# Another table of queue orders for a two-layer diffusion backbone on one core

## The chip, the core and the metric

The kernel runs on one NeuronCore of one Trainium2 chip. A core has five engines that run side by side, each through its own list of instructions in order: TensorE (PE, matrix multiplication, with weight loads shown as PEld), VectorE (DVE), ScalarE (ACT), GpSimd (POOL) and SyncE (SP, which here only issues DMA transfers). They wait for each other by semaphores. The metric is device microseconds of the program on that core; lower is better. The kernel before took 1788.57 us (median of three runs, 1785.81 to 1789.31).

## The reference

Two layers over 512 latent tokens and 256 context tokens, 1024 features, all in float32:

```python
# layer 0: neighbourhood attention (8 heads) beside spatial gating, one output projection
q, k, v, u, g = jnp.split(h_lat @ w_in, splits, axis=-1)
a_lat = neighbourhood_attention(heads(q), heads(k), heads(v), heads(kc), heads(vc), rpb)
s_lat = spatial_gating(jax.nn.gelu(u), jax.nn.gelu(g), w_s, b_s)
y_lat = jnp.concatenate([a_lat, s_lat], axis=-1) @ w_out
# layer 1: two-way retention with 8 heads; its state starts from the context
y_lat = retention_output(outs_lat[0] + outs_lat[1], g, gn_g, w_out)
# after each: a gated MLP with a convolution over three tokens
a = dwconv3(h @ w_in, conv_w, conv_b)
gate, up = jnp.split(a, 2, axis=-1)
return (jax.nn.silu(gate) * up) @ w_out
```

Every part is normalised before and after, and shifted, scaled and gated by `silu(c) @ ada_w + ada_b` (called ada below).

## The kernel before

Each float32 operand of a large product is split into a high and a low part that TensorE reads in one pass; a product is then three matmuls (high by high, high by low, low by high, lines 216, 217 and 218 in the helper `mm3`, line 215 where a single helper line issues all), which add into one tile of PSUM. ScalarE writes the high part (line 171) and VectorE the low part (line 172).

The stages follow each other: the start (ada of the first norm, tiles `ad`, lines 266 to 289; transposes of the input, tile `ht`, line 1831; the projection `ug`), spatial gating, attention, output projection, the first MLP, retention, the second MLP. Matmuls of a stage have one width: 512 columns for `ug`, `wf` and `wr`, 256 for `px`, `rn` and the scores, 384 for the first MLP.

Four small kinds of PE instruction differ from these:

- In attention, `weigh` (lines 1144 to 1151) multiplies the transposed weights by the values in plain float32, into a PSUM tile `o` of which one half of the matmuls writes partitions 0 to 63 (lines 1144, 1146, 1148, 1149 and so on as `lo`) and the other half partitions 64 to 127 (`up`): ten instructions a head. Each is recorded as two passes.
- For the context tokens the same function issues four such matmuls a head into `oc` (line 1167), two into each half.
- The first ada products (`ad`, line 266) are in plain float32 too, 32 instructions with two passes each.
- Rows of ada results are turned into columns by transposes with two or four rows (`at` in line 370, `adt` in line 276): 64 instructions.

All other transposes have 128 rows.

The order in which an engine issues is not the order of the Python code. After everything is built, `queue` (line 1849) takes each engine's list, decodes a table `ORDER` for it, and chains the instructions in the order of the table:

```python
for e in LANES:                      # PE, DVE, Activation, Pool, SP
    lane, at, last = lanes[getattr(mybir.EngineType, e)], -1, None
    for _ in lane:
        ...                          # one number z of the table
        at += 1 + (z // 2 if z % 2 == 0 else -(z + 1) // 2)
        if last is not None:
            self.tc.add_manual_dep(lane[at], last.name, sync, reason="queue")
        last = lane[at]
```

A number of 0 means "the next one of the program's own order"; others jump forward or back. The table holds 10,880 places for PE, 2,299 for DVE, 1,746 for ACT, 458 for POOL and 400 for SP. Tiles have their addresses before the table is read, and what waits for what follows from the data and the addresses.

Of the kernel before, what the change touches and what calls it, by code (L numbers as in the profile page):

```python
# [2045 lines left out]
```

## Time and profile before

| | |
|---|---|
| time, median of three runs | 1788.57 us (1785.81, 1788.57, 1789.31) |
| profiled execution, first to last instruction | 1784.0 us (4.6 us under the median; its time as the runs count it is not listed) |
| PE busy | 1748.3 us |
| DVE, ACT, POOL busy | 1388.2, 1017.5, 340.1 us |
| DMA, mean | 142 GB/s |

Times in the profile count from the first instruction. A row of the list in order of time gives the start, the time of one or several merged instructions, the engine, the line, the tile written and the tiles read, the shape (rows by columns of the weights, then what is written) and the count. Matmuls are pipelined, so the time that one takes from the engine is read from the start of one to the start of the next and not from its own duration.

### The profile page before, as it was taken

To read this page: it belongs to the slowest core of one execution; us is meant where nothing else is said; L and a number is where in the kernel's file an instruction comes from. 1 tells how busy PE (TensorE), PEld (TensorE's weight loads), DVE (VectorE), ACT (ScalarE), POOL (GpSimd) and SP (SyncE) were. 2 spreads that over 40 slices of the span, in tenths; PEclk is the share of its full clock that TensorE was granted. 3 is DMA by queue.
4 is the path that set the end of the run, shared out by engine and by line. 5 is a ranking of instruction groups with operands and counts; after the bars stand their busy time and mean duration, and the time that the engine had idled before them with its cause. 6 is when DMAs were issued, how large, how long until landed. Compare 5 with 4: busy or idle time off the path is not lost.

```text
span 1784.0 us, 28774 instructions
## 1 busy us (share of the span) xinstructions
PE 1748.3 (98%) x11024; PEld 1578.7 (88%) x11024; DVE 1388.2 (78%) x2363; ACT 1017.5 (57%) x1882; POOL 340.1 (19%) x462
## 2 busy tenths in 40 slices
PE   7999999999999999999999999999999999999997
PEld 4898888799998999999899998998999789999996
DVE  3887886898887787889867666666655799998887
ACT  6633567776555555655665434433444577766773
POOL 1101322230132322222221001101001200222221
PEclk9999999999999999999999999999999999999999
DMA  8345331364687877886734332332322235887764
GB/s 304 116 133 165 99 110 45 106 180 118 171 174 174 173 174 155 164 178 161 257 126 125 118 113 71 119 95 81 97 71 60 107 122 147 214 216 185 180 145 130
DMA packets 84398, 253.44 MB, mean 142 GB/s; under 512 B 11026, under 2 KB 11538, under 8 KB 84260
## 3 DMA queue, kind: packets, MB, share of 16 engines
q1 hardware_dynamic: 55044, 191.27, 33.7%
q0 software_dynamic: 26912, 51.95, 17.1%
q10 hardware_dynamic: 2304, 8.39, 1.2%
q8 instruction: 86, 1.41, 0.3%
q14 instruction: 52, 0.43, 0.1%
HBM read 191.80 MB, written 39.85 MB: 130 GB/s over the span
## 4 chain that ended last, share of the span: by engine, by line
PE 89%; DVE 5%; ACT 3%; DMA 1%; issue 1%; POOL 1%; SPq 0%; DVEq 0%; POOLq 0%; ACTq 0%
PE px L215 11%; PE wf L216 4%; PE wf L217 4%; PE wf L218 4%; PE rn L217 4%; PE rn L216 4%; PE rn L218 4%; PE py L215 4%; PE px L216 2%; PE px L217 2%; PE px L218 2%; PE py L218 1%; PE py L217 1%; PE py L216 1%; PE ug L216 1%; PE ug L217 1%
## 5 line engine op out<-in xcount | busy, mean ns | idle before, releaser
L326 DVE SCALAR_TENSOR_TENSOR acc<-ar,cs,acc 128x512 f32<-128x512 f32 x256 | 190.5, 758 | 11.1 <-DMA ar<-in_adaw 4.3
L216 PE MATMUL rn<-rwv,h0c 128*128 128x256 f32 x384 | 107.8, 281 | 0.0
L217 PE MATMUL rn<-rwv,h0c 128*128 128x256 f32 x384 | 107.5, 281 | 0.0
L218 PE MATMUL rn<-rwv,h1c 128*128 128x256 f32 x384 | 107.2, 280 | 0.0
L1734 POOL DMA_DIRECT2D yf<-yp x64 | 56.0, 963 | 265.1 <-ACT yp L1730 237.7
L1574 ACT ACTIVATE pre<-px 128x256 f32<-128x256 f32 (+2 forms) x160 | 56.0, 369 | 78.0 <-PE px L215 55.9
L1587 DVE SCALAR_TENSOR_TENSOR cv<-pre,cw,cv 128x769 f32<-128x769 f32 (+1 forms) x88 | 77.3, 882 | 27.5 <-ACT cv L1586 26.9
L1586 ACT ACTIVATE cv<-pre,cw 128x770 f32<-128x770 f32 (+1 forms) x88 | 80.9, 925 | 21.5 <-DVE g L172 11.4
L1730 ACT COPY yp<-wf 128x512 f32<-128x512 f32 x118 | 68.4, 584 | 41.8 <-PE wf L218 34.2
L215 PE MATMUL px<-blk,wb 128*128 128x384 f32 (+1 forms) x480 | 79.2, 309 | 1.1 <-ACT pre L1574 1.1
L215 PE MATMUL px<-hs,wc 128*128 128x384 f32 (+1 forms) x480 | 78.9, 309 | 1.0 <-ACT pre L1574 0.8
L1590 DVE SCALAR_TENSOR_TENSOR cv<-pre,cw,cv 128x769 f32<-128x769 f32 (+1 forms) x88 | 76.8, 881 | 0.9
L215 PEld LDWEIGHTS px<-hs,wc 128*128 128x128 f32 x480 | 73.5, 188 | 4.1 <-ACT pre L1574 1.6
L215 PEld LDWEIGHTS px<-blk,wb 128*128 128x128 f32 x480 | 72.8, 188 | 3.8 <-ACT pre L1574 1.6
L171 ACT ACTIVATE wc<-q 128x512 fp32r<-128x512 f32 x80 | 49.8, 629 | 44.1 <-PE py L215 20.7
L216 PEld LDWEIGHTS rn<-rwv,h0c 128*128 128x128 f32 x384 | 72.4, 189 | 1.2 <-issue 0.2
L218 PEld LDWEIGHTS rn<-rwv,h1c 128*128 128x128 f32 x384 | 72.5, 189 | 0.7
L217 PEld LDWEIGHTS rn<-rwv,h0c 128*128 128x128 f32 x384 | 72.4, 188 | 0.9
L1734 POOL DMA_DIRECT2D yd<-ypg x48 | 48.4, 1053 | 122.1 <-ACT ypg L1730 104.6
L218 PE MATMUL rn<-rwg,h1c 128*128 128x256 f32 x256 | 71.3, 279 | 0.0
L217 PE MATMUL rn<-rwg,h0c 128*128 128x256 f32 x256 | 71.1, 279 | 0.0
L216 PE MATMUL rn<-rwg,h0c 128*128 128x256 f32 x256 | 71.1, 279 | 0.0
(1545 smaller groups left out, 6328.4 us busy)
## 6 DMA issues: line engine op xcount, KB each, us to landing
ar<-in_adaw SPq DMA_DIRECT2D x96, 512.0 KB
yf<-yp POOLq DMA_DIRECT2D x64, 256.0 KB, 4.3
yd<-yp POOLq DMA_DIRECT2D x54, 256.0 KB, 5.5
yd<-ypg POOLq DMA_DIRECT2D x54, 256.0 KB, 5.5
fin<-xd SPq DMA_DIRECT2D x8, 512.0 KB
xn<-in_x SPq DMA_DIRECT2D x6, 512.0 KB
xb<-in_x SPq DMA_DIRECT2D x6, 512.0 KB
xd<-xb ACTq DMA_DIRECT2D x6, 512.0 KB
```

What stands on the lines that cost most here:

```text
L171: self.S.activation(hi, src, AF.Copy)
L215: mm = lambda *p, **k: self.T.matmul(*p, skip_group_check=True, **k)
L216: mm(out, lhs[0], rhs[0], start=first, stop=False)
L217: mm(out, lhs[0], rhs[1], start=False, stop=False)
L218: mm(out, lhs[1], rhs[0], start=False, stop=last)
L326: V.scalar_tensor_tensor(out=acc[s], in0=raw[:, kk * 512 : kk * 512 + 512], scalar=self.cs[:, 8 * s + k : 8 * s + k + 1], in1=acc[s], op0= ...
L1574: S.activation(pre[:, i, c : c + w], ps[:, b : b + w], AF.Copy, scale=scale)
L1586: S.activation(d, s, AF.Identity, scale=w1, bias=b)
L1587: V.scalar_tensor_tensor(out=d[:, 1:W], in0=s[:, 0 : W - 1], scalar=w0, in1=d[:, 1:W], op0=ALU.mult, op1=ALU.add)
L1590: V.scalar_tensor_tensor(out=d[:, 0 : W - 1], in0=s[:, 1:W], scalar=w2, in1=d[:, 0 : W - 1], op0=ALU.mult, op1=ALU.add)
L1730: S.copy(v, ps)
L1734: G.dma_start((yd[t] if first else y[t])[:, o], v, accum_op=ALU.add)
```

## The change

Only the string `ORDER` is replaced:

```diff
 LANES = ("PE", "DVE", "Activation", "Pool", "SP")
 ORDER = """
-c-p;Nd8{4RS^wtDnSI~x+<kxd?Yp1-{1(SsV#izD_}N+P#Ez4YCUKi4X_Is#ZBx`#Ep3Bn)0P4)sBEQz3Mx<wv>*_mB2>|Tsf0u&{s0Li{@`D}Gt
...
+c-pmld7LCyec$g@RaaG4Rd-k4_ch%;)6?B^-}il=yL0c%?(FQ&>}sWD?^D{<2|_|b2q6#%fk7YvLI&A@!5D0e!6Cka1-26$?8HuR91{Bz+lk}EIliyD_d
...
 """
```

Decoded, both tables are permutations of the same five lists. The new one was found by a search over a dependence graph with durations from the trace. Counting decoded places:

| | PE | DVE | ACT | POOL | SP |
|---|---|---|---|---|---|
| instructions | 10880 | 2299 | 1746 | 458 | 400 |
| at the same place in both | 2445 | 560 | 497 | 207 | 271 |
| mean distance moved, places | 7.9 | 2.7 | 2.2 | 1.0 | 0.6 |
| last ones that are the same | 443 | 96 | 71 | 20 | 18 |

On PE, stretches of neighbouring instructions with the same output tile and the same operands number 5,901 in the old table and 8,628 in the new one: matmuls of different tiles alternate more often. An example, the end of attention's first head (tile, operands, count of neighbours):

```
old                              new
o0  <- ptall,vn0    x7           py1 <- h0a,wv1      x2
pq2 <- h0a,wq2      x1           o0  <- ptall,vn0    x1
pq2 <- h1a,wq2      x1           py1 <- h1a,wv1      x1
o0  <- ptall,vn0    x2           ...
pt04<- ident,sc04   x4           s14 <- ka10,q10     x1
s13 <- ka10,q10     x1           o0  <- ptall,vn0    x1
s13 <- kb10,q10     x1           s13 <- kb10,q10     x1
s13 <- ka10,q10     x1           o0  <- ptall,vn0    x3
o0  <- ptall,vn0    x1           pt04<- ident,sc04   x1
```

How the four small kinds lie in the PE order, as runs (neighbours of the same kind):

| kind | instructions | runs, old | runs, new | runs of one, old | runs of one, new |
|---|---|---|---|---|---|
| `o` (lines 1144 to 1151) | 80 | 10 | 44 | 1 | 30 |
| `oc` (line 1167) | 32 | 9 | 18 | 0 | 11 |
| `at`, `adt` (lines 370, 276) | 64 | 27 | 50 | 4 | 40 |
| `ad` in plain float32 (line 266) | 32 | 7 | 16 | 2 | 9 |

The first instructions change as well. On PE the old table begins with four transposes `ht` and the new one with four `ad` matmuls; on SP the load of the ada weights `ar` for them stands fifth in the old table and third in the new one, ahead of the second half of the context tokens and of the identity.

More of the change, by code (lines that the diff above doesn't have):

```diff
@@ L122 @@
-@@jnir@}1y(!nhI2}$&4xY17X=?f*L*8Ly-vy5P21TRGeD1$d^=(V`)4&hg#kS#~<5WSTVkAQtL1=HwHw8KLBcv4fdZ*wSe{^br$9er@DL?`=`?k
-h2|gTV?ivhS}Zr@Z()lO2;2{4e{KrGx
+c-pmld7LCyec$g@RaaG4Rd-k4_ch%;)6?B^-}il=yL0c%?(FQ&>}sWD?^D{<2|_|b2q6#%fk7YvLI&A@!5D0e!6Cka1-26$?8HuR91{Bz+lk}EIliyD_d
+??EAFi1`s=E5sd%ySleShEY?^P3FlNBNXe>RC!B8OoRB@;<aH^`8q9wM)gf&rCuBBx!EW&RbHldLToA;RfoX!tZVG#DjA_xXK}nrdA$c*{x8#G+&~b}n5
+$6liO`dWBA(N+#(1;y(A2tk3D{=8cRDQ&-p1?D*vPT*~W89lS(MIQkN!7a4Eew=<2lPs|gY?d~~s`dKy*=;&2z6Fb)qj{9gkHbnQ+&#@0P-jUC-2U%lNB
@@ new lines @@
+YlXyz}jX$!ZK~{d~c@Q*|tcELOC*O^L!5{oxcBpa~Pk5K|jJSY*TFd5!T*I18KV8qK5c1#-!TGP-HyonjUfq_+G@J2QY4uP0D3q7prL)sIEkw5xLt>p1v
+bB{#rbIRF$DrI=)LY_*!2olCO=&;uMMYQ_Wa@a41AHp36{rFr7*h)eOVvL>bzpi8SrD_{S$aUNUKQZFLRT8?31&D#pjDE<Tx{dnOxTj?<@V8mPptAH#QX
+-fE_epIqO5e36z)S)$rj$HscGfO)WHO_0j7MqXPWk;H2#JX+UrmohQi7N+64;NrgVi3iz3%ybjA7t5#C;}UgLz+NJmr5d6t%I1i_jGZ|<OfY6~@$4DmXJ
+^+Mv$^a>Ah=pX)?n!FPqE$*cal(eyMLg6-~b)mI@p~e+M(xJpQiIanj8{D*+!im379NHYTgTT)Kkvs!+%pGYW-FG%`!G@?DY^%4#MyhPLQ2sva9^FhF0Q
+!%16sRlKXXedIA*Y?@X(O2kz&NPJEcgOYD7&teIBJu^?N`;rr#QUB4E_2#(Xkj7n_}yp@%x!8#5jRIRPT5~-Ki!z{JQhgL(dITdr58^eKjzs|nKsPQc)-
@@ new lines @@
+*U2r4ixF^85oM_^0SPdV;9QJ&-^xfR-n1rIhux-jB88#muPr|sDHrv7%#m<)l~Zh;oCyIY<U`=h!iGZlYCEi@xWE?Qbf<N_ptp-@feZSR6{*I$j<j5ygt
+c(4N>%E_GvuR`o@dwIwohUCxidz+0_DdpP<$@D*k{y!CDR<c!F&gn%xVBr~_U@4S&eAFJRnPu3q_LM)ma%vR}X+-TzrOn{1eUlHp+CI2^X2>vcAhse%)u
+r?c7fvo+JX8bS+or4*d|?iu_?u3bk5#)yuscrhkxT#qo?Uqav<J5G<Y$Cw}rOHZ*rTK_Ej3^Vs|dLst{#1JJ2J~3_CDHMiJ!UqbmDO#Rr?;!G&hCH#R{(
+<!(e0r27#)*d}wz*lNeMD-air^Qtljgk{q)w`!4!w=Nm79el!b)|C-plAS?6d4?Mu*F@^N{c=qs4{!Z?ZFI>1*s?vEO4$YtgYo%dpBI=Jq$(<P=fxb@o-
+p=jt%kzlVLEUHvetp~6yA?q&7}TQ04vyuh@NaW}i3yF#>)qziw}PL3}fJ@Rq3haN|sX76T{q<ioCB>NQFxp47Cwt+d%k&?f9C8x+$)ireH18ig68WdvYf
@@ new lines @@
+baUT<L_kOW@EH4^j5*YeXgUgw~gpy>_xWs471>qfE?7@hu7tmP#8wrnh4apJH{u*k0PWI5}sJ$;8tDJ7S33rMcC{^Y;oTrjnmZR)FfF5O8e4hKFU7A_@i
+u)ox`7H>hNL9Zl7Y034h7_|H$Z_!r*T)dY7P)`B&D7f5iCQzs#Nx=x{^Jqrz|Vqi%YgJubY=`UzhhX?~r3liT?y4Q~x?!AA$-$YWn-2e%I$*xWh%5P<v&
+-S-G$YyZ-vk20#h^g&iNe>Kk|4pUBJ^*sKEw?4|7J{*@79gsv}CDAw&3VRFnOI4>|U>Imi^TiABOAepbCWwQP%`?FO5TR>8qxl6Y4fHqAZCe1a;)jF5mp
+aNvI=Mj$z8ap5_^I90Mp>hUs#@Dxse=RQ{KWVKT&yc#^9FkR6uCQ{qJeh^PY6~FmqRqtLyKWbw!X~1&**yyp8vxBBRXG|`4je#FbimvY~%qXh3HlGFWGB
+|HI+Wje80jhu<~)NYbwK7zLrB5N2n0L_Gum?K-nmTmQV9@53SJ~wn!At(5;4pLF}};0u2}@%*dfml9d?R4N#^kBS%Q9EgJ#fDRpV&pw=RdF16NDbq(@6M
@@ new lines @@
+|w5Zxl<i>kr7jJt>l%ccycDwObtpa(rT#A!%^4ia=LVlnp+}XzQdE0-<KTBz__V&ust0_M8PWY`n2Kkx|}9uoSsaT-&IxaZdGP=EqCu42WH9TRAjf6Xp>
+H7ICRIb%*tz0KwG$42)WRXoS=jgRyzGS+j)w8jsXy6t*}^c_yqed+oXlp5$Jh-orcAXWuK+?$n|Ud-NE*b_NvWGL&Q<1yC*^KVox#Ze~Dcw3=N)|I^lVN
+eTeyy&g#5xxu4$0X6Cq;KFiMLzR14EPM!WfAb>{4o@O5sUJ%Zn*=MeC1jF_i8)*53GQ?nt5rqMtfBpn=EB<(dQn-ZF)<9czl?3BHvP1_q0epLK<$>lF`c
+3vP%7F;VCS{AOhd#%56Qv$6aDKaJ;pBKtI+Y#Jo@AQ??`OPc1YGOYDSq#E5uTH;m6iU1>I}_V4W(1DwN5z4_MzI2c4Qk+7Rs!54DPLWQ2*Zg20h8@c6gK
+?-Z`A@>g*yX&myUGws9@n*ag?mgA!(5!G);!3X;rhLlRxKCed9o-80Sh;`;bT68((?PtwdZ&w%@K7xsbLXf4%V+OiTKCymFB%YZfn-jM~k&VkP``eT+~p
@@ new lines @@
+sIh({tuh3%{<FyX6Sz~o*IyL@>DAd)iuEIs!Z7dEVs}@)H!3q3e@p__I5BrM`IHwG(^{~`=|?1;&Hn0;`3*Q7xz)l13EW*FiWiqn&B91lWZ<T1m_ANa+^
+(@`+P+BH>`VuBA7ubMDzC`$l%q!SJ`i{uj6rO+axdl4uzWuoaPg37}1kdh1M>Q+e8lD*M#;;b@$#Epte{b8VQHA`S-F>u!Fv5*yT(608Gf4v~urKVWl}$
+hfE}=C}YO}k-};O@$+!rQ9iWYy<k8CpL8tkr>%pWpg7`vyR)BTk1|@w&(0n1p3O|pq*~iDfN!lWojO#vl1lGiAaFao8VI(J?01_pou)f;3V5+dq(rD|i2
+B>%d374~tS5U4&KQ^#kPCC{&4FNza*{PO?e7TBlNnV_PKS|{8+-%(6vlZR<d?EwM3Ym8=DZ&7Xp66z)=1B{wuKJRWxDV|)*WiPu<gg}T}A-+q|(o@De@n
+<c;R9o)^_foSsUnk9~&ARB1v<*XZze9P4_2s?Lpz40;!x)z!*SK$|MKDE&#esA|6$l_70@-!K28@A7e7L?|`Fjb#-o2Ug>P{hhUP&ner5~o-V`HF1#I_H
@@ new lines @@
+f1zC%#NlxA8@4lFY4O4H6P^+a^;mw9<(p*D5d8YJVtsJ@t2D<&f)UeD?i6DC+oC%U=xHT*V~~~WvY@Ed8R@S3{_p@EPD_jI?+bWV3kP%;3LvVn{aX<^=E
+UQ`UZ5^BAHH&;;~|+E$bvr%9sU;dOab|F~R6GJr3puSB5LLuQVdGS6Txyt*wJ~wMq01o-)DSXw9zjKk_8k7hVDLv$*Z(7HrX52Lbn1_BQ5na<a%TnxRXV
+6EyG)<09$3OxK>VFl5^bm~!+qTF=I9xY|dz9ct9{3y1yy=?Jb5E^>GWbKM+;$rAP;kPI2BI_^=aRGZ_5`8XmEQZg7wr7^5x;mTENs7FQxB@UlCn<7W>)C
+NcX=qc*yXh+^@Zxh2v-qkhbByAzQPw47YAr`hKIu*p%3`LLN=!yBz>RAeKtn~R~@!6W{KJs)P%_HWVvt86a<Do-OutL#rm`Im_hR8X3H|X3#VI+L*>Xo4
+`lgFChKHNi{wE%}L99Y^9cmo4)g9PwMrVen$j&{sp*C*N8NHpC|_kz#RR#`&1W}`V*Natx03C*s0WT)#{47e_)FHhp-uF2<^vo7X@{%M*YSVovM-Bsu5c
@@ new lines @@
+!oV-c+xa{wY9C6n>9N!JQDGYj*+uweI&Tv#u>^gLG-mW*D1)P_0+`4D!Dq5ZoSLD$o?J#3G{int%_%9%<JwReI0NUcR9H}`U)6mEWX;)Ju+M@Y(0+I&u;
+<$ydEe5fN$^CL5rLZJqrgQ&;1X86fRTMeOxWlA`~d*yW8TyMQ}!e+Kn+K2`!h~-P?7q?2a|Bd<&F>7P$&Le(d;L8Fz91<^4;!Y_%mQ_%jvX0U1F}?TH$h
+CwDsdT}JoiX|DaqeUxcGa<upIB=BT*Ztnf;1ML0m0nTdtVc-b(Sg55Qw4uL;6j?Ea{j{-u-05m=EF#m{inM(E7zFN>tII36%$dx>d<!)S)N<}BxCWp8yi
+6_lq*TYPCaZaTTpIw8xj~A^FdW79j_DRB^e`tkXU-1Rk0D0glo@pQW7s3ZD`ue3p-E&>k(>36mQb~-St9>)>=(h&6X6h=zh}HEX-RIR%1JmB4{LiW3?1d
+8Seq-0k#~f`?q&Dt#TXc5Gf1g6<RgK{IE>O0Nl;&+P>e)*A)+C-pVuPLS|r*Ppw6!70R;9~6j5Gm3$#bU)m-6L7iUmF#)kR^D4tehq?P+=f_Eq!LRTP0p
@@ new lines @@
+_Sk=LX0v(qu0~&4mL5qN$bacorRO_tF#e4$1&`{rj*N0@C5mLfCEk<eY&0?hpsjDIZ_ntwghG{kWPhKLgDB%AKJ$J;uJ(Rh@}<?IxJzE?H}MTffgja-j(
+Hn{;Qo;P5wgzJrs*{(JEy+FxGBF%)rT7CsN$dNjl-BD`z44ik5gU-i6dL;zazO+#v4wKAEc$cs9J$O6gFt4(Hl_xP(9Ju7J|U0V;FJyH0Q>?+Y|;qcwiW
+a*O%4)|u&<Y2d)0at-J4a&ZPB^D=|YEOieG_BbPp{8O~Pp&r7MDw;~yEQ#WDIp4^g8=E50dH@p`Cbw9&2gDirpxNcG%J6p{&~YbHBQLL%YXCoW<Fy^1-&
+?BV$u<x~p2aYVkvs^tkxbIMMFA;azhKpU3V~WG_sgj1^m@{O<?cC?mt?GKR?|YK-(rj;MJyCcp5(%pcs(fvOLIWsf_`Z5_CCOUlyX(X?W-KhROmOr5fiO
+(ii6zea{dmxNbshOg@0t~&L?2eBS#PZDmzNsuY#Su%I2N+-)CI6$l4wU?d#Xpf0^C9&MR!rJ2z`?^VINC`7mS`aYly+L2`b;I{Gwrcu*}o%|^g}`rm`2^
@@ new lines @@
+W`SmTHAJ;USsr^>_6e)e`WL<+xHmjqMJ1Wo|ovJyWuzQWUsKk(;SFS(rJ2>!J<$aABMZ*tb6Z!AB*2dTx8R^^Za{v-}4}&@I7~Pk9f<;a&?ISVvphUcUs
+-z*%WdYa9VlyhRsrp{MBy7siuc`xOhF1mm5*=S+k3N1bFbovvfm@hNI2+2UHO++*l=_&aRuSR$H!QVKT1(-OzFUn+HIc;#=fg5-daN)}+c4#k&Uj)hS*)
+LS7jLHMaMSj#+PMaA+{GL;Y|N98T=<gOyquPq*kEuFrweii-%8U>F1~ScwfF?CL?d*{VJxTIDp*weg7;*+D$$B_{CN058@Y+MW|=eCzzV^XERs$UaU}GQ
+GgI57Ew${tAPHps^P%<9(V9ANw?B>3_5T#RxX%*!np(NT=xR8UFq}P0=s0FR)=8q4N{3vnbl6Ghbz2VdrP2&wNOD1*+x|>%rssG3e?2Ao%n!OCQAp{(O~
+R=1_!ZC|*cFRBnHp{XW-1yvk;6U7bYj9UQ<~!P;7^S`oK7{+t!rUqCW!Bh5sx@{(f}eTnTLr}=#c;0*cCqlZ@go7dQQ-KO@;flcns6IS7lt_El68TPx(s
@@ new lines @@
+y4O03vtxk@_TG%sby-iv8j<KK;m=}T%*z>E>tF9wQsQN7z}!~@506Th553;+4vg!b@n^#V6<xgJ_k*oh{ca#qU~z&7!6G7_Y|mC8sRg8xdArxU~G^(?Y!
+-t?sD@J<GgVMn<jfnHEzT^6nC8LR@j5qw%)9L+$?}v)DnIq*+z#z>oBsR7udm}W&=dC;zzT4fw@^2a2!N!;r)!}pizj{R=F?o?NjWNj82d>X3Pui9Nxh*
+(J!<8AQ+rc9D{&cKhGoe;fiMcsT*8TeZ#?)D|C@Z3yt191O(h@hdF!R*hDjCz?x_x=bK+-$0`JlS?{}VYE3%FpYFSH(%shc`PX=_$3{8uS-$bJZbzn~iD
+6Y*8Xgjb@s;VB{ZlkK)!ox=OqC13yl@Uy)(e(uU0|#{wgvbGFWn)xuj{ads4A5*|7}|?%j+;?95~@o97eesUUpGI6#56?D3-edK?W4wY_v%lr3s~68`!s
+q%dYV1<o@2in@w`jXDtYPmC>I;9PzpkUHb?2VM|~99Q!-Aw)zmuzl{M*5PJLnfkC$aJv&#TkFqoMP~AM{X#61_7{h<hF6`D;+=N#hkr?-`a<2I;*zb4Q-
@@ new lines @@
+>{l;G2cfwLG#9{#G7unOPKEn^ljm`{jOU|=bvwbc8TA%+k5M685$~c_om;?{?jjK#i-YMw+xWDnOkqbkTtbGcDoEuK7X$Aj<a66!flO^EN4Cn2vJ^L<<V
+LJg&&Q%GPsQWNW-_%l@%*!-9#hA3;nBWKdv{;EtM4yYqM&mmLMZJ1KMn5Bj=66J>PDUi8tH$sQ#S&8KdivZ^S|2%)jSnH_`hTC%C7PT6ofZ!v?iF!EHB;
+l*6e-sqV%n>o?Dt6X!97*5ZO?Y&h;*1t!UY*vhtcYp~WaYxxafNN)2DY_Ng_+Z@#Cz~&(?&u3}j^NhnJ|L8S#&jc?DmlF=2cqy#%HH6}qxeWgjl<1>)^X
+1A1yjuA6N~!AWK;I&Ljg=2`U(49b$3Mud=z4|`Un+9^CZ2wcIev>-O912nlvUW1Wpq6GeLsK8^3Pk}NB+G=p7*eG+|*a-@ILNAkCo5jJdVDNr$1oOgL6O
+4r*GLty7Pl{YMq{A-8Zqm`OTgB*-GCy;kBsaovvA9$qY(Z>)mBm$Dgs?53+zK9<=w(z;5uJ)(ULUsUfH|e1IHvYJ^6mnNjFcYvFFTqD|J{7+gQHE&rrZ%
@@ new lines @@
+WlRwfCCnW+xg8xI^3EzqV@pS(0))h3sY~XvEDX|O6P0uRQe4FvbxgEC2q;$KUNMx8iS4|TTPYBF<Xk8k`zx>2sy$<k<XnzBfg8JEP3YSk>tI-q`~k0yLF
+2c(mqHyX3&CbNffQ$cym6_>9iz9$gL9sk25cLnPE}13NwV(Ly}Zrdl;;&1o)GW|18-8E9@FP$oc6WOoq>G`mt;1qVvXKs|*q>=Xlr-DoDOjOt^Dp)~X!b
+q=UDV#~nw6Hxx`NlBBu8MvZTNPmnC$5-k=rM>4&wVe7ZYLgiw2UK%f4+(=ZptqP;HRCf8SFa;!AIE1u_WE2VmXH+}?*h-#ui>+wos+!Kh(ZO?vWqWSo8~
+v{2+?$KBI==*Qc);{n4*~NIn_23oLX(A?AKIjwMk(*y_Q|bNt@?pk{^6WoF%16Wbx`fFSa3PLl7S0gUR;>&iZ}9Q8UGvhD!--HwL82^z5RZ?+dsXns%ZU
+;9w%C(x{dOSf@OxABd7?2%0swglB8P{kvlQ$MD+gwsN`eu
```

125 lines of the change are left out of this document (55 added, 70 removed).

## The prediction

> **What bounds the kernel now.** I read the page first, then the busy times by stage, then TensorE's waits, then single stretches of TensorE's work in order of time.
>
> ```profile
> span 1784.0 us, 28774 instructions
> PE 1748.3 (98%) x11024; PEld 1578.7 (88%) x11024; DVE 1388.2 (78%) x2363; ACT 1017.5 (57%) x1882; POOL 340.1 (19%) x462
> PE 89%; DVE 5%; ACT 3%; DMA 1%; issue 1%; POOL 1%; SPq 0%; DVEq 0%; POOLq 0%; ACTq 0%
> ```
>
> TensorE is busy for 98% of the span and carries 89% of the chain that ended last. So an order can gain in one way only, by filling TensorE's idle time, 1784.0 - 1748.3 = 35.7 us, and the slow time behind it. It loses whatever makes TensorE's own work longer. The stages:
>
> ```profile
> 0.00:44.60 44.60, 34.19 (x167) 18.86 (x168) 17.32 (x35) 28.75 (x62) 6.90 (x20) 1.00 0.85 304
> 178.40:356.80 178.40, 173.54 (x1157) 144.03 (x1157) 143.97 (x385) 120.08 (x294) 48.12 (x70) 1.00 0.28 90
> 401.40:624.40 223.00, 219.11 (x1139) 202.64 (x1139) 180.63 (x253) 131.87 (x232) 50.52 (x68) 1.00 0.69 162
> 1382.60:1471.80 89.20, 82.98 (x555) 75.46 (x554) 77.95 (x140) 57.05 (x117) 12.62 (x21) 0.96 0.34 114
> 1471.80:1739.40 267.60, 267.60 (x1893) 249.94 (x1893) 241.08 (x377) 187.41 (x337) 55.28 (x65) 1.00 0.73 181
> 1739.40:1784.00 44.60, 35.05 (x201) 30.40 (x199) 32.42 (x50) 17.78 (x37) 8.38 (x11) 0.95 0.42 129
> 1420.00:1430.00 10.00, 6.12 (x31) 5.03 (x29) 10.00 (x21) 9.27 (x21) 3.78 (x7) 0.72 0.53 207
> ```
>
> The columns are the stretch, its length, then busy time and count of PE, PEld, DVE, ACT, POOL, and the granted clock. PE's idle time is 10.4 us at the start, 4.9 in attention (178 to 357), 3.9 in the first half of the first MLP, 6.2 where retention passes into the second MLP, 9.5 at the end; all other stages together 0.8. The last row shows one more cost: the clock stands at 0.72 around 1425, behind the second longest wait:
>
> ```profile
> PE ht L1831 <- DVE xn L425: 10.1, 2, 8.1
> PE ht L552 <- ACT sa L560: 3.1, 1, 3.1
> PE wf L216 <- ACT yp L1730: 2.9, 2, 1.7
> ```
>
> The columns are who waits for whom, the total in us, the count, the longest.
>
> **The change, part by part.** Instructions and durations are the same; what changes is which stand side by side. Between ordinary matmuls this costs nothing: inside a tile and from tile `stc` to `stl` below the pitch is 0.12 us for 256 columns alike. The four small kinds are another matter.
>
> *Rows with two or four partitions (`at`, `adt`).* One alone, then four together behind four `oc`:
>
> ```profile
> 1192.82 0.28 PE L216 MATMUL stc<-rv,kd 128*128 128x256 f32 x1
> 1193.03 0.22 PE L370 MATMUL at<-ident,arow 2*128 2x2 f32 x1
> 1193.40 0.28 PE L218 MATMUL stc<-rv,kd 128*128 128x256 f32 x1
> 1193.52 0.28 PE L216 MATMUL stl<-rv,kd 128*128 128x256 f32 x1
> 1193.64 0.28 PE L217 MATMUL stl<-rv,kd 128*128 128x256 f32 x1
> 238.85 0.28 PE L218 MATMUL px<-h0a,wk 128*128 128x256 f32 x1
> 239.06 0.66 PE L1167 MATMUL oc<-pcT,vn 128*64 128x128 f32 x8
> 239.87 0.28 PE L217 MATMUL px<-h1a,wk 128*128 128x256 f32 x1
> 240.08 0.41 PE L370 MATMUL at<-ident,arow 2*128 2x2 f32 x4
> 240.75 0.28 PE L1066 MATMUL s<-ka,q 128*128 128x256 f32 x1
> ```
>
> From 1192.82 to 1193.40 are 0.58 us for two matmuls of 0.12 and one transpose: 0.34 for it. From 239.87 to 240.75 are 0.88; less 0.12 and 0.23 (the pitch of 512 columns, below) this leaves 0.53 for four. So each further one costs 0.06 and each run 0.28. The table goes from 27 runs to 50: 23 x 0.28 = 6.4 us.
>
> *`oc`.* From 238.85 to 239.87 are 1.02 us, less 0.24 gives 0.78 for four in a run. They go by pairs, one for each half of the partitions, and a pair takes two passes of 0.11; so 0.43 is work and 0.35 the cost of the run. The table goes from 9 runs to 18: 3.2 us. A matmul that lost its partner takes a pair's time; counting pairs in the new order adds 1.2. Sum 4.4 us.
>
> *`o`.* The pairs of a run, and one alone:
>
> ```profile
> 233.61 0.43 PE L1144 MATMUL o<-ptall,vn 128*64 128x256 f32 x1
> 233.62 0.43 PE L1145 MATMUL o<-ptall,vn 128*64 128x256 f32 x1
> 233.88 0.38 PE L1144 MATMUL o<-ptall,vn 128*64 128x256 f32 x1
> 234.09 0.38 PE L1144 MATMUL o<-ptall,vn 128*64 128x256 f32 x1
> 234.96 0.27 PE L1148 MATMUL o<-ptall,vn 128*64 128x128 f32 x1
> 235.06 0.27 PE L1148 MATMUL o<-ptall,vn 128*64 128x128 f32 x1
> 215.84 0.28 PE L1066 MATMUL s<-ka,q 128*128 128x256 f32 x1
> 216.05 0.43 PE L1151 MATMUL o<-ptall,vn 128*64 128x128 f32 x2
> 216.41 0.39 PE L1066 MATMUL s<-ka,q 128*128 128x256 f32 x1
> 216.63 0.28 PE L1067 MATMUL s<-kb,q 128*128 128x256 f32 x1
> ```
>
> Two halves start 0.01 us apart, so they run side by side; a pass of 256 columns takes 0.21 and one of 128 takes 0.10 to 0.11. The lone one takes 216.63 - 215.84 - 0.24 = 0.55, of which 0.21 are its two passes: 0.34 for the run (I take 0.30, what remains of a run of ten). The table goes from 10 runs to 44: 34 x 0.30 = 10.2 us. Partners are torn apart too: a lone one of 256 columns takes two passes, 0.43, as a pair does. Pairs counted in both orders, this adds 6.1. Sum 16.3 us, the largest term.
>
> [...]
>
> *`ad` in plain float32.*
>
> ```profile
> 27.15 3.11 PE ad L266 x14
> 31.23 0.40 PE L216 MATMUL ug<-ug,h0a 128*128 128x512 f32 x1
> 31.55 0.59 PE L266 MATMUL ad<-ar,cs 128*2 128x256 f32 x2
> 32.08 0.50 PE L217 MATMUL ug<-ug,h0a 128*128 128x512 f32 x1
> 32.41 0.39 PE L218 MATMUL ug<-ug,h1a 128*128 128x512 f32 x1
> ```
>
> In a run each takes 2 x 3.11 / 14 = 0.44 us; alone 32.41 - 31.23 less two matmuls of 0.23 leaves 0.72. So a run costs 0.28, and 7 runs become 16: 2.5 us.
>
> Together 29.6 us more work for TensorE: 21.7 of it inside attention (`o`, `oc` and 1 of the transposes'), 3.3 at the start, the rest spread thinly. Nothing hides it, except TensorE's own idle time.
>
> *What comes back.* At the start the new order puts `ad` ahead of transposes that wait 8.1 us for `xn`, and fetches its weights earlier. I take 2 us of the 10.4, since what follows is dense. In attention idle time and stretched pitches are about 8.6 us (4.9 idle, the rest from my sum of pitches); a slower TensorE gives the others time, so I take 6. Waits of the first MLP (3.9, the `yp` buffers): 1.5. At retention's end four transposes waited 3.1 us for ACT, and the clock of 0.96 over that stage's 89.2 us cost 3.5: the new order has these transposes among the last `wr` matmuls, and I take 5 of 9.7. The end: none, since the last 443 entries of PE and the last ones of all other queues are the same. On DVE, ACT, POOL and SP entries move by one to three places; where their engines are under 95% busy this hides behind TensorE, and I cost it at nothing; if that cover fails it shows as new PE waits, a rival below. Sum: 14.5 us.
>
> Against the profiled execution: 1784.0 + 29.6 - 14.5 = 1799.1. The median lies 4.6 above that span, so 1803.7; I say 1803.
>
> **Bounds.** Low: all idle and slow time outside the end and the first 6 us is filled, some 32 us, and the 29.6 stand: 1786. High: nothing is filled: 1788.6 + 29.6 = 1818.
>
> **Rivals.**
>
> *Faster:* the lone small matmuls overlap with their neighbours after all. For it speaks that the search used durations, and that few lone ones exist in the old order to measure by (1 of `o`, 2 of `ad`, 4 of the transposes). Against it: all seven cost 0.28 or more beyond their passes. At no cost of a run the time is 1788.6 - 14.5 + 7.3 (lost pairs) = 1781; it decides below 0.10 us a run. Chance 0.16.
>
> *No change:* the search's gain is as large as the unseen cost, because idle time is nearly all filled: 1788.6 + 29.6 - 29 = 1789. For it: a search minds just those waits. Against: 8.1 us at the start are a load and a norm, and the end is the same. Chance 0.12.
>
> *Slower still:* tiles stay open longer, as their matmuls alternate with others, and ACT and DVE get results late and in bunches; PSUM has four, two and two buffers by tag. In the second MLP, where DVE is busy for 241 of 267.6 us, such waits are not made up. With 8 us of new waits and 6 less filled: 1817. [...] Chance 0.15.
>
> *My forecast:* 0.57, 1793 to 1813.
>
> **How the numbers follow.** About 0.2% (3.6 us) is what a measurement can tell from no change: under 1785.0 is faster, over 1792.1 slower. Slower: 0.57 + 0.15 = 0.72; same 0.12; faster 0.16. The range for 8 in 10 leaves out most of the faster case and the worst of the slower still: 1785 to 1817.
>
> **What would show it.** In the new profile `o` and `at` appear as lone rows with about 0.34 us beyond their passes, and attention lasts some 16 us longer with TensorE busy throughout. PE's busy time exceeds 1748.3 by 20 to 30 and its idle time falls from 35.7 to 20 or 25. The clock no longer dips near 1425. I am wrong if lone rows cost no more than rows in a run, or if the idle time falls by more than 25 us or grows.

## The result, and the profile after

The new table makes the kernel slower: 1815.99 us median of four runs (1815.02 to 1818.24) against 1787.19 us for the old one (four runs, 1784.77 to 1789.31). The medians differ by 28.8 us; the ratio is 1.0169, 95% interval 1.0157 to 1.0181, which is 28 to 32 us. The forecast was 1803, 1793 to 1813; the measured time lies above that and within the wider range of 1785 to 1817. The profiled execution of the new kernel took 1818.24 us; its span is 1816.5 us, 32.5 us over the span of the old profile. All numbers by stage below are of these two profiles. Of the runs further down, one of the four executions of e3 took 4477.5 us for a reason that its record does not show, and it is left out of e3's times.

The page of the new kernel, busy times:

```profile
span 1816.5 us, 28887 instructions
PE 1787.1 (98%) x11024; PEld 1577.2 (87%) x11024; DVE 1393.5 (77%) x2363; ACT 1027.2 (57%) x1882; POOL 343.6 (19%) x462
```

PE is busy for 38.8 us more than before (1748.3), and idle for 29.4 us in place of 35.7: 38.8 - 6.3 = 32.5.

To see in which stage, both spans are cut at the same work and not at the same time. Both kernels issue the same 10,880 PE instructions, so a stage ends where instructions worth the same sum of pitches have been issued. The old kernel by such stages (columns as in the prediction: stretch, length, busy time and count of PE, PEld, DVE, ACT, POOL, clock):

```profile
0.00:35.30 35.30, 24.89 (x120) 12.61 (x121) 10.00 (x22) 23.18 (x52) 6.90 (x20) 1.00 0.82 289
35.30:156.40 121.10, 121.10 (x723) 103.17 (x722) 100.96 (x172) 56.61 (x99) 13.63 (x24) 1.00 0.49 155
156.40:373.10 216.70, 211.84 (x1377) 177.71 (x1375) 172.39 (x430) 143.11 (x345) 59.18 (x83) 1.00 0.31 98
373.10:619.80 246.70, 242.81 (x1279) 226.45 (x1279) 203.65 (x288) 150.44 (x265) 57.13 (x78) 1.00 0.70 167
619.80:903.70 283.90, 283.32 (x1490) 257.64 (x1489) 242.25 (x354) 171.88 (x318) 72.37 (x95) 1.00 0.75 180
903.70:1404.00 500.30, 500.07 (x3545) 464.80 (x3544) 322.59 (x571) 217.53 (x329) 56.64 (x71) 1.00 0.31 95
1404.00:1474.80 70.80, 64.58 (x431) 58.77 (x431) 65.60 (x110) 52.57 (x110) 10.59 (x17) 0.95 0.39 131
1474.80:1784.00 309.20, 299.65 (x2073) 277.60 (x2071) 270.77 (x422) 202.19 (x370) 63.66 (x76) 0.99 0.68 174
```

The new kernel, the same work:

```profile
0.00:35.70 35.70, 27.33 (x120) 11.60 (x121) 11.62 (x25) 23.78 (x53) 7.14 (x20) 1.00 0.82 301
35.70:159.30 123.60, 123.60 (x726) 101.53 (x725) 98.47 (x168) 55.86 (x96) 12.00 (x23) 1.00 0.46 142
159.30:401.10 241.80, 237.28 (x1373) 179.97 (x1372) 173.89 (x431) 145.42 (x348) 64.66 (x85) 1.00 0.29 91
401.10:645.10 244.00, 243.23 (x1280) 226.24 (x1279) 203.88 (x288) 152.62 (x264) 55.54 (x77) 1.00 0.69 169
645.10:932.30 287.20, 286.59 (x1490) 256.80 (x1489) 242.76 (x354) 174.00 (x319) 72.80 (x95) 1.00 0.75 180
932.30:1436.50 504.20, 503.80 (x3544) 465.45 (x3544) 325.09 (x571) 218.24 (x327) 56.14 (x72) 1.00 0.30 96
1436.50:1507.00 70.50, 65.45 (x432) 59.12 (x431) 65.98 (x111) 51.32 (x109) 11.77 (x16) 0.95 0.32 109
1507.00:1816.50 309.50, 299.78 (x2072) 276.49 (x2070) 271.82 (x421) 205.97 (x371) 63.55 (x76) 0.99 0.68 175
```

Line by line (length; PE busy; PE idle, which is length less busy):

| stage | length | busy | idle |
|---|---|---|---|
| start | +0.4 | +2.4 | -2.0 |
| ada products up to attention | +2.5 | +2.5 | 0 |
| attention | +25.1 | +25.4 | -0.3 |
| first MLP, first part | -2.7 | +0.4 | -3.1 |
| first MLP, second part | +3.3 | +3.3 | 0 |
| retention | +3.9 | +3.7 | +0.2 |
| passage into the second MLP | -0.3 | +0.9 | -1.2 |
| second MLP and end | +0.3 | +0.1 | +0.2 |

Attention is 25.1 of the 32.5 us. A lone `o`, in the new kernel's list of PE in order of time:

```profile
217.49 0.28 PE L262 MATMUL py<-h0a,wv 128*128 128x256 f32 x1
217.61 0.28 PE L263 MATMUL py<-h1a,wv 128*128 128x256 f32 x1
217.82 0.65 PE L1191 MATMUL o<-ptall,vn 128*64 128x256 f32 x2
218.39 0.39 PE L264 MATMUL py<-h0a,wv 128*128 128x256 f32 x1
218.62 0.28 PE L262 MATMUL py<-h0a,wv 128*128 128x256 f32 x1
```

From 217.61 to 218.62 are 1.01 us; two matmuls of 0.12 and two passes of 0.21 leave 0.35 for the run.

### The profile page after: what moved, and what is told of

Same layout as the page of the kernel before. It is cut to its first block, busy times and chain, and to the rows that moved or that the text cites. A ratio compares the mean times of both kernels' runs of the same rounds, so it can differ in the third digit from the quotient of the medians.

```text
span 1816.5 us, 28887 instructions
## 1 busy us (share of the span) xinstructions
PE 1787.1 (98%) x11024; PEld 1577.2 (87%) x11024; DVE 1393.5 (77%) x2363; ACT 1027.2 (57%) x1882; POOL 343.6 (19%) x462
## 5 line engine op out<-in xcount | busy, mean ns | idle before, releaser
L261 PE MATMUL px<-hs,wc 128*128 128x384 f32 (+1 forms) x480 | 113.3, 309 | 0.4 <-DVE hs L218 0.3
L261 PE MATMUL px<-blk,wb 128*128 128x384 f32 (+1 forms) x480 | 112.3, 309 | 0.1
L263 PE MATMUL rn<-rwv,h0c 128*128 128x256 f32 x384 | 106.1, 281 | 0.0
L262 PE MATMUL rn<-rwv,h0c 128*128 128x256 f32 x384 | 104.7, 283 | 0.0
L261 PEld LDWEIGHTS px<-hs,wc 128*128 128x128 f32 x480 | 83.4, 188 | 6.7 <-ACT pre L1620 0.8
L261 PEld LDWEIGHTS px<-blk,wb 128*128 128x128 f32 x480 | 81.9, 188 | 5.9 <-ACT pre L1620 0.4
L264 PE MATMUL rn<-rwg,h1c 128*128 128x256 f32 x256 | 70.8, 280 | 0.0
L263 PE MATMUL rn<-rwg,h0c 128*128 128x256 f32 x256 | 70.5, 279 | 0.0
L261 PE MATMUL py<-blk,wc 128*128 128x384 f32 x240 | 69.5, 338 | 0.0
L261 PE MATMUL px<-hs,wd 128*128 128x384 f32 x240 | 68.7, 339 | 0.0
```

The costliest lines, as they stand in the source:

```text
L261: mm = lambda *p, **k: self.T.matmul(*p, skip_group_check=True, **k)
L262: mm(out, lhs[0], rhs[0], start=first, stop=False)
L263: mm(out, lhs[0], rhs[1], start=False, stop=False)
L264: mm(out, lhs[1], rhs[0], start=False, stop=last)
```

## Experiments

In what follows a kernel is old or new by its table, and times are medians beside the old kernel's runs on the same chip.

**Which stage: the two tables joined at the end of attention.** Each hybrid takes one table up to the cut and the other one for all instructions that are left.

```diff
 e1: attention and all ahead of it   old order
+    all behind it                   new order
 e2: all behind attention            old order
+    attention and all ahead of it   new order
```

> All five queues follow the old table up to the end of attention (everything that the profile of before starts in its first 373 us) and the new table from there on. The two profiles, set side by side at equal amounts of TensorE work, differ by 28.0 us at the end of attention and by 32.5 at the end of the span, so the new order costs 4.5 us behind attention. Theory A (the loss lies in the four small kinds, nearly all in attention, and the stages behind it get hardly any idle time back): about 1787 + 4.5 = 1791, 1789 to 1794. Theory B (the alternation of ordinary matmuls costs time by itself; five sixths of it lies behind attention): 1787 + half of 29 or more, over 1800. Theory C (the prediction's own give-back holds behind attention: +4.6 for runs, -6.5 for waits of the first MLP and of the passage into the second): 1785.

Measured: 1787.55 against 1786.12 us, ratio 1.0009 (1.0000 to 1.0019).

> The reverse: the new table up to the end of attention (what the profile of after starts in its first 401 us), the old one from there on. Theory A: 1787 + 28 by the two profiles, less what a run differs from a profile: 1811 to 1815. Theory B: 1787 + 14 or less, under 1802. Theory C (start +1.3, attention 21.7 - 6): 1787 + 17 = 1804.

Measured: 1815.65 us, ratio 1.0164 (1.0149 to 1.0179). So +1.4 and +29.5 us: the loss lies in attention and ahead of it, all of it. Theory B is out: behind attention stand most of the alternations of ordinary matmuls, and the new order costs next to nothing there. The new kernel's trace shows it directly too: from 401 to 1436 us, matmuls of 256 columns among their like follow each other after 0.117 us within a tile and 0.118 us across tiles on average, those of 384 columns after 0.176 us both ways. e1's 1.4 us are below even theory A's 4.5, in part because in e1 the passage took 68.6 us against 70.5 in the new kernel, with the clock at 0.98 against 0.95. They lie between theory A's 4.5 and theory C's 2 us of gain; it is e2 that speaks against theory C, with 1815.65 for 1804.

**The price of a torn run, by itself.** The old table with one small kind torn, the ordinary matmuls where they were:

```diff
 e3, the first head's o:
-o0 x7, pq2 x2, o0 x2, pt04 x4, s13 x3, o0 x1
+o0 x1, pq2 x1, o0 x1, pq2 x1, o0 x1, pt04 x1, o0 x1, pt04 x1, o0 x3, pt04 x1, o0 x1, pt04 x1, o0 x1, s13 x3, o0 x1
 e7, one group of at:
-pk0 x2, at06 x4, pv0 x11
+pk0 x2, at06 x1, pv0 x3, at06 x1, pv0 x3, at06 x1, pv0 x3, at06 x1, pv0 x2
```

> The old table with one thing of the new one: the ten o matmuls of a head are cut into the same pieces as in the new table (44 runs in place of 10, 30 of them of one, members in the new order), with one regular matmul or transpose between two pieces. 97 of 10,880 places on PE change; the other four queues are the old ones. Theory A: 34 runs x 0.30 + 6.1 for lost pairs = +16.3, so 1803.5; up to 4 more if each run costs 0.37, as the new profile's lone rows suggest (1807). Theory B: a place or two moved costs nothing, 1787 to 1790. The rival of the prediction (lone ones overlap with their neighbours): 1787 + 6 = 1793.

Measured: 1805.06 us (three runs, 1805.05 to 1806.53) against 1786.12, ratio 1.0109 (1.0089 to 1.0129), +18.9 us between the medians and 19.5 by the ratio. Attention in e3 (its PE was busy for 211.84 of 216.70 before):

```profile
155.50:392.10 236.60, 228.99 (x1377) 180.24 (x1376) 171.93 (x430) 143.33 (x345) 58.63 (x83) 1.00 0.28 90
```

Busy +17.2, close to the 16.3 of the prediction, and idle 7.6 in place of 4.9: +2.7. A hundred moved instructions make two thirds of the loss, and they make waits besides: in attention `pt` now waits 1.0 us for DVE's `sc` and 0.9 us for ACT's `arow`. That this comes of the last piece of an `o` ending later is likely, and was not tested.

> The old table with the two- and four-row transposes at and adt cut into the pieces of the new one (27 to 50 runs), three regular instructions between two pieces, 116 places on PE changed. By the prediction's price of 0.28 for a run: +6.4, so 1792.5 (1791.5 to 1794). [...]

Measured: 1793.24 against 1785.79 us, ratio 1.0043 (1.0029 to 1.0057), +7.5 us. The page of e7:

```profile
PE 1755.2 (98%) x11024; PEld 1578.4 (88%) x11024; DVE 1389.4 (77%) x2363; ACT 1016.8 (57%) x1882; POOL 339.4 (19%) x462
```

PE's busy time grew by 6.9 us for 23 runs, 0.30 each; the prediction had 0.28. So the prediction's faster rival, which needs less than 0.10 us a run, is out for these kinds.

What of a small kind makes the cost of its run was not shown: no run here changes the shape alone, and `o` and `oc`, on half the columns, are in plain float32 besides. Not every narrow kind has such a cost, see the last section.

**All torn, nothing else.** The difference between this kernel and the new one is what the rest of the new order is worth.

```diff
 e11: o and at, adt as in e3 and e7, and oc, for instance
-oc0 x4, pq2 x3
+oc0 x3, pq2 x1, oc0 x1, pq2 x2
```

> The old table with o, oc, at and adt cut into the pieces of the new one (44, 18 and 50 runs); ad keeps its 7 runs, and everything else stands as in the old table (231 places on PE changed, the other queues the old ones). By the prediction's prices 16.3 + 4.4 + 6.4 = 27.1 us more than 1786.5: 1813.6 before any waits; e3 and e7 measured 19.5 and 7.5 for o and at, adt, so with 4.4 for oc 1817 to 1818. The new kernel differs from it by everything else that the new order does, plus 2.5 us for ad. If the rest of the new order gave back 14.5 us, as the prediction says, this kernel would stand at about 1816 + 14.5 - 2.5 = 1828. Theory A (the rest gives back next to nothing net): 1813 to 1819, level with the new kernel.

Measured: 1819.65 against 1786.13 us, ratio 1.0187 (1.0173 to 1.0201), +33.5 us: above theory A's range by a hair and well under 1828. Page and attention of e11:

```profile
PE 1778.6 (98%) x11024; PEld 1585.0 (87%) x11024; DVE 1388.7 (76%) x2363; ACT 1017.6 (56%) x1882; POOL 339.4 (19%) x462
158.30:401.30 243.00, 235.04 (x1377) 181.43 (x1376) 172.26 (x430) 143.33 (x345) 58.88 (x83) 1.00 0.28 87
```

Busy +30.3 where the prediction's prices say 27.1; the rest of the 33.5 is waiting. Torn runs in the old order make attention 243.0 us long, and the new order 241.8. So in attention all the rest of the new order is worth 1.2 us; in the whole kernel 33.5 + 2.5 (`ad`) - 28.8 = 7.2 us by the medians, and 1817.8 + 2.5 - 1816.5 = 3.8 us by the spans of the two profiles; the 2.5 is the prediction's price, which no run took by itself. The prediction had 6 and 14.5.

**The new table without torn runs.** In e4 the runs of the new order are closed again; e6 does the same with the few that the old order tears.

```diff
 e4, the first head's o:
-py1 x2, o0 x1, py1 x5, ..., o0 x1, ..., o0 x1, ..., o0 x3, ..., o0 x1, pq2 x1
+py1 x2, ..., o0 x10, py1 x2
 e6, one group of at:
-stc4 x2, at17 x1, stc4 x2, ..., rn41 x4, at17 x3
+stc4 x2, at17 x4, stc4 x2, ..., rn41 x4
```

> The new table with o, oc, at and adt put back into one run for each tile (o 44 to 8 runs, oc 18 to 8, at and adt 50 to 20); the plain-float32 ad of the start stays as in the new table, and so do the other four queues and the alternation of all ordinary matmuls. 829 places on PE change. Theory A: by the prediction's prices 17.2 (o) + 4.8 (oc) + 8.6 (at, adt) = 30.6 us less: 1816 - 31 = 1785, somewhat less if each run of o costs 0.37 (1782). Theory B: the alternation is still there, so above 1805. If the new order had filled waits of attention at all, this kernel should come out under the old one by that much.

Measured: 1794.75 against 1786.12 us, ratio 1.0047 (1.0032 to 1.0062): 21 us better than the new kernel, 10 less than expected, and still over the old one.

> The old table with o, oc, at and adt in one run for each tile, 343 places on PE changed, nothing else. Theory A: 10 fewer runs, by the prediction's prices 3.2 us less: 1783. Rival (a later run is a later result, and waits as in e4's attention take the gain): 1786 to 1789.

Measured: 1784.18 against 1785.79 us, ratio 0.9992 (0.9983 to 1.0001): 1.6 us less, half of what was expected and not told from nothing by its interval. Attention in e6 and in e4, whose small kinds lie in equally many runs:

```profile
156.30:372.70 216.40, 210.48 (x1377) 177.29 (x1376) 171.98 (x430) 143.13 (x345) 58.47 (x83) 1.00 0.32 98
158.80:384.50 225.70, 215.66 (x1373) 175.60 (x1372) 174.11 (x431) 144.55 (x348) 65.24 (x84) 1.00 0.30 97
```

At equal runs the new order is 9.3 us longer in attention. PE is idle for 10.0 us there in place of 5.9, and busy for 5.2 us more. By an estimate from pitches summed in the two traces, about half of these 5.2 us lies at 128-row transposes and the matmuls beside them, which the new order mixes more, and a quarter at ordinary matmuls among themselves. No run tests this part. The waits of e4 in that stretch:

```profile
PE pq L258 <- ACT vt L1069: 2.0, 2, 1.4
PE pt L1178 <- DVE at L214: 1.9, 5, 0.7
PE pt L1202 <- DVE sc L1131: 1.7, 3, 1.1
```

So the new order, with closed runs, fills no wait of attention; it has more of them. The new kernel differs from e4 only in how its small kinds lie, and its idle time there is 4.5 us: the time that torn runs take covers these waits, which is why its idle time looks as small as the old one's. Whether the other four queues' order makes these waits, or the place at which e4 closes the runs, was not told apart.

**The passage into the second MLP.** The prediction expected 5 us back there. Three rows of the new kernel's PE waits, and the stretch around them, first in the old and then in the new kernel:

```profile
PE pf L263 <- DVE hb L218: 2.0, 1, 2.0
PE pf L262 <- ACT hb L217: 1.9, 1, 1.9
PE pf L264 <- DVE wp L218: 0.8, 1, 0.8
```

```profile
1421.00:1424.00 3.00, 0.38 (x5) 0.41 (x5) 3.00 (x9) 3.00 (x8) 0.54 (x1) 1.00 0.84 330
1427.00:1430.00 3.00, 2.61 (x13) 2.32 (x12) 3.00 (x5) 2.37 (x5) 1.50 (x2) 0.50 0.55 216
```

```profile
1451.00:1454.00 3.00, 2.36 (x12) 1.64 (x10) 3.00 (x8) 3.00 (x9) 0.01 (x1) 1.00 0.47 173
1454.00:1457.00 3.00, 0.39 (x1) 0.19 (x1) 3.00 (x8) 3.00 (x9) 1.98 (x3) 1.00 0.01 5
1460.00:1463.00 3.00, 2.23 (x11) 2.00 (x10) 3.00 (x6) 2.56 (x6) 1.82 (x2) 0.50 0.74 247
```

In both kernels DVE and ACT are busy for all of the 3 us in which PE waits. The new order does put the `ht` transposes among the last `wr` matmuls, and the wait moves from them to the next step, the copies `hb` that DVE and ACT make of their results. After two gaps of 1.9 and 2.0 us with one matmul between them the granted clock is 0.50 from 1460 to 1463 us, as it was before from 1427 to 1430 after one gap of 3.1.

What keeps the two engines busy is also a matter of their own order. In the new kernel ACT takes the squares `jxd` of other rows while PE waits for `hb`:

```profile
1452.97 0.63 ACT L449 ACTIVATE jxd<-xd 128x512 bf16<-128x512 f32 x1
1453.59 0.63 ACT L449 ACTIVATE jxd<-xd 128x512 bf16<-128x512 f32 x1
1454.20 0.45 ACT L606 ACTIVATE sa<-ht,ab 128x128 f32<-128x128 f32 x1
1454.54 0.63 ACT L217 ACTIVATE hb<-sa 128x512 fp32r<-128x512 f32 x1
```

Whether ACT and DVE could serve `hb` sooner in another order was not tried. To test whether DVE and ACT are the bound, their work on retention's rows was cut in the old kernel, which then leaves it out for all but 64 of every 512 columns:

```diff
 def gated_rows(self, r):                       # e8 and e10
+            if r["name"][0] == "d":
+                h = slice(h.start, h.start + 64)
             self.V.tensor_tensor(out=y[:, h], in0=y[:, h], in1=gate[:, h], op=ALU.mult)
 def residual(self, r, last):                   # e8 and e10
+            c = slice(h.start, h.start + 64) if r["name"][0] == "d" else h
-            self.V.scalar_tensor_tensor(out=xt[:, h], in0=y[:, h], ..., in1=xt[:, h], ...)
+            self.V.scalar_tensor_tensor(out=xt[:, c], in0=y[:, c], ..., in1=xt[:, c], ...)
 def ssq(self, src, name, n):                   # e10 alone
+        if name[:2] in ("yd", "xd"):
+            junk, src = junk[:, 0:64], src[:, 0:64]
```

> The old table; the multiplication by the gate and the residual sum of retention's four token tiles are done on 64 of every 512 columns only, the rest of them is left out. That takes some 9 us off DVE between 1403 and 1428 us, nothing off PE. Theory D (the idle time where retention passes into the second MLP is set by DVE and ACT, DVE being busy for 10.00 of the 10 us from 1420, so no order of TensorE's work fills it): the waits of 3.1 us for sa and of about 1.2 us for hb and wp shrink or go, and the low clock behind them with them: 4 to 7 us less, 1779 to 1782. Rival (the order on PE or the arrival of wp sets it): 1785 to 1787.

Measured: 1784.20 against 1785.79 us, ratio 0.9990 (0.9982 to 0.9999). The wait for `sa` fell from 3.1 to 2.4 us only; the expectation failed.

> As e8, and the sums of squares of retention's four token tiles, on ACT, are taken over 64 columns of every 512 too; the rest is left out. Theory E (the passage is bound by the serial chain of row statistics, gates and residual sums on ACT, POOL and DVE, which the chain of waits of before follows from 1404.66 to 1428.74 with no PE in it; in e8 only DVE's links were cut and ACT was then busy for all of the 10 us): the chain loses 6 us or more, the wait for sa (3.1, 2.4 in e8) falls under 0.5 and the low clock behind it goes: 4 to 6 us under the old kernel, 1780 to 1782. Rival (the order on PE or the arrival of wp sets it): no better than e8, 1783 to 1786.

Measured: 1783.94 against 1786.56 us, ratio 0.9987 (0.9979 to 0.9996), 2.6 us less, under the 4 to 6 expected; in its profile the passage takes 68.4 us in place of 70.8. The wait for `sa` is still there:

```profile
PE ht L552 <- ACT sa L560: 2.4, 1, 2.4
1418.00:1424.00 6.00, 3.21 (x24) 2.58 (x22) 5.60 (x15) 5.35 (x13) 1.99 (x4) 1.00 0.66 250
```

So the rows' chain is a part of it, and behind it stands the next piece of work on the same two engines (`sa`, `hb`), still 5.60 and 5.35 of 6 us. Theory E is right in direction and too simple in size. Neither run shows whether an order of the queues would fill the gap.

**A version under both kernels.** e5 takes from each table the stages where it is the shorter, and closes the runs.

```diff
 to the end of attention                old order
+then two fifths into the first MLP     new order
 then to the last wr products           old order
+then to the first of the second MLP    new order
 the rest                               old order
+o, oc, at, adt                         one run for each tile
```

> The old table, with the new one where the curve of loss in e1 fell: the new order from the end of attention to two fifths through the first MLP's stretch (e1 gained 4.0 us on the old order there) and from the last wr products to the first ones of the second MLP (2.1 us gained), the old order everywhere else; then o, oc, at and adt are put into one run for each tile (o 10 to 8 runs, oc 9 to 8, at and adt 27 to 20). Theory A (stages add, and a run costs 0.28 to 0.37): 1786 - 4.0 - 2.1 - 3.2 = 1777, 1774 to 1780, under both kernels. Rival (what a stage gains is taken back by the next, or later small kinds make new waits as they did in e4's attention): 1783 to 1787.

Measured: 1781.01 against 1785.79 us, ratio 0.9972 (0.9961 to 0.9984), 4.8 us less than the old kernel (3 to 7); half of the 9.3 forecast, and between the two ranges of the expectation. The gain is where the new order had its one clear success, the first MLP's first part:

```profile
373.00:616.50 243.50, 243.30 (x1279) 226.06 (x1279) 204.15 (x288) 153.44 (x266) 56.99 (x78) 1.00 0.70 170
1399.20:1469.70 70.50, 65.30 (x431) 59.09 (x430) 65.92 (x111) 51.34 (x109) 11.77 (x16) 0.95 0.33 110
```

243.5 us against 246.7, with 0.2 us idle in place of 3.9. The passage keeps its 70.5 us; the 2.1 us of e1 were not repeated.

**A search that counts the runs.** e9 goes on from e5 with a search of the same sort as the one behind the new table, with a cost for each run.

```diff
 from e5's order
+500 places on PE, 329 on DVE, 159 on ACT moved; small kinds in as many runs as in e5
```

> The order of e5 changed further by a search over the same dependences, now with a cost of 0.28 to 0.35 us for each run of a small kind and with the pitches read from the trace; it moved 500 places on PE, 329 on DVE, 159 on ACT against e5 and kept the small kinds in 8 runs of o, 8 of oc, 20 of at and adt, 7 of ad. By the search's own account it starts with ad (-3.1 us by the end of the first 40 us), drops a wait ahead of attention (-2.0) and smaller ones (-4.3), and finds next to nothing where retention passes into the second MLP (-0.6). Theory A (with the runs' cost counted, an order search gains on this chip too): 1781 - 9.3 at the most, 1772 to 1777. Rival (its gains are as little to be had as those of the new table): 1779 to 1783.

Measured: 1822.59 against 1786.56 us, ratio 1.0199 (1.0185 to 1.0213), +36 us. Its page, and its longest waits on PE:

```profile
PE 1761.9 (97%) x11024; PEld 1582.1 (87%) x11024; DVE 1391.5 (76%) x2363; ACT 1020.7 (56%) x1882; POOL 344.0 (19%) x462
PE px L223 <- ACT pre L1582: 5.9, 4, 3.1
PE rt L1398 <- DVE rg L1386: 5.0, 4, 3.5
PE py L223 <- ACT pre L1582: 4.2, 2, 3.9
```

Neither theory had this. The span is 1820.8, so PE is idle for 58.9 us, where e5 has 32.1: the runs are those of e5, and waits came that the search did not see, where DVE and ACT deliver late. PE's busy time is also 14.7 us above e5's 1747.2, with a mean clock of 0.991 in place of 0.996. Which dependence or duration its model lacked was not found.

## Why the prediction was right or wrong

The direction, the stage and the mechanism of the loss were right: torn runs of small kinds, nearly all in attention, as lone rows with 0.35 us beyond their passes. What failed is the give-back. The size was half: 15.1 us from span to span in the sum, 32.5 in the profiles and 28.8 between the medians. PE's work was put 9.2 us too low (29.6 for 38.8) and the give-back, some of it slow time, 8.2 too high (14.5, where idle time fell by 6.3); that is the 17.4 between 15.1 and 32.5. Step by step:

- *`at`, `adt`, 6.4 us:* e7 measured 6.9 of busy time. Right.
- *`o`, 16.3 us:* e3 measured 17.2 of busy time in attention. Right in work. What was missed is 2.7 us of new idle time in e3.
- *All torn together:* busy 30.3 in e11 where the prices of the three kinds sum to 27.1, and 33.5 with the waits; 6.4 us too low.
- *Start, 3.3 less 2:* idle time fell by 2.0 as forecast; work grew by 4.9 up to attention, not by 3.3. The table's own runs of `ad` (9 more) and `adt` (6 more) at 0.28 would have given 4.2.
- *Attention's idle time, 6 of 8.6 us back:* **the step that failed.** Idle time went from 4.86 to 4.52. "A slower TensorE gives the others time" was argued and not read: in the old order, e3 and e11 have a slower TensorE and more idle time (7.6 and 8.0 us). In the new order it does cover waits (10.0 us of idle time in e4, 4.5 in the new kernel), but these are more than the old order had, so nearly nothing is gained on the old kernel.
- *Passage, 5 of 9.7 back:* **failed too.** Its length went from 70.8 to 70.5. The prediction's own row for 1420 to 1430 had DVE busy for 10.00 of 10 us and ACT for 9.27; the step read the clock and PE in it, and not those two columns. That the work of these two engines holds PE up there is shown in part only, by e8 and e10.
- *First MLP, 1.5:* 2.7 came back, better than forecast. *The end, none:* right.
- *Ordinary matmuls alternate at no cost:* e1 puts all behind attention at +1.4 us, first MLP and passage included. In the second part of the first MLP and in retention the new kernel is 7.2 us longer, of which e7's torn `at` make 2.9 + 1.6 = 4.5 in the same stages (286.8 and 501.9 us); so some 2.7 us in 790 are left for alternation and waits. Nearly right there. In attention e4 has 5.2 us more busy time than e6 at equal runs, for which the prediction had no term.
- *From span to median, 4.6:* in every later run the time exceeds the span of the same execution by 1.8 us, and the old profile's 1784.0 fits the run of 1785.81. With 1.8 the forecast would have been 1801, so 2.8 us of its nearness are luck.

Of the signs named, attention grew by 25.1 us and not by 16, PE's busy time by 38.8 and not by 20 to 30, idle time is 29.4 and not 20 to 25, and the clock's dip did not go, it moved to 1460. The rival "slower still" (8 us of new waits, 6 less filled, 1817) came nearest in number, in part by luck: that less is filled is right, and e4 shows new waits, but the new kernel's idle time did not grow, more busy time makes up the rest, and the rival's place, the second MLP, is the same in both kernels.

## What to carry to other kernels

An order can lose more by tearing instructions that run cheaply side by side than it can gain in waits (here 33.5 us lost in e11 and 3.8 to 7.2 given back by the rest of the new order): count the runs of each kind with its price before looking at any wait, and give a search that price. Before idle time of one engine is entered as a gain, read the other engines' columns in the same stretch; where two of them are busy throughout, do not count on an order of the first to fill it. And a new order's give-back is measured by a kernel that has only its cost (here e11), not by the idle time of the new kernel, which its own cost covers.

## What was not expected of the hardware

Not every narrow matmul shows a price for its run. Behind the start, `ad` is computed with weights of four columns, and the new kernel alternates them with full ones:

```profile
40.05 0.40 PE L264 MATMUL ug<-ug,h1a 128*128 128x512 f32 x1
40.28 0.28 PE L314 MATMUL ad<-ah,c 128*4 128x256 f32 x1
40.40 0.40 PE L262 MATMUL ug<-ug,h0a 128*128 128x512 f32 x1
```

From 40.05 to 40.28 are 0.23 us and from 40.28 to 40.40 are 0.12: just the two pitches. So this one costs nothing beyond its pitch, and the same two steps are 0.22 to 0.24 and 0.11 to 0.12 us at eight of the nine other lone ones in the new kernel. A lone `ad` of two columns in plain float32 costs 0.28, by the prediction's rows at 31.23 to 32.41 us. Which of their differences decides was not tried.

An order's effect in a stage hardly depended on what stood ahead of it: behind the new order of attention, the old order of e2 took 246.5, 284.0 and 500.3 us for the first MLP's two parts and retention, against 246.7, 283.9 and 500.3 in the old kernel. And the clock's dip at the passage comes and goes with little: the passage had a mean clock of 0.95 in the old kernel, the new one and e5, with PE idle in it for 6.2, 5.1 and 5.2 us, and 0.98 in e1, e3 and e4, with 4.6, 7.2 and 4.6.
